# Gate projection of a float32 decoder trunk by one level of Strassen, gate and up with x loaded and weights streamed, their product transposed for down

## The chip, the cores and the metric

One core of one Trainium2 chip runs the whole program. The metric is device time in microseconds (us) from launch to end. TensorE is called PE, VectorE DVE, ScalarE ACT, and SyncE, which issues the loads, SP.

## The reference

Two layers of a decoder trunk on 256 positions, all in float32: four attention groups merged by one output projection, then a dense SwiGLU FFN with hidden width 5632. What matters here is the FFN:

```python
h = rms_norm(x, ffn_norm)                       # x: 256 x 2048
x = x + (silu(h @ w_gate) * (h @ w_up)) @ w_down    # 2048 -> 5632 -> 2048
```

## The kernel before

x lies transposed in SBUF, features on the partitions: X0 to X7 hold two feature tiles of 128 each, by 256 positions, and XS0 to XS7 hold the same, times the norm's gain, split into a high and a low part. Every float32 product is made of three products of such parts in PE's fp32r mode: high weight by high x, high weight by low x, low weight by high x.

The weights come from HBM in the order of use as tiles `raw` of 128x2048 (1 MB; L208 issues the load, three buffers). Each is split in two halves of 1024 columns: ACT rounds a half to `wh` (L216), DVE subtracts to get `wl` (L217). wh and wl have four buffers each.

In the FFN the weights are stationary. `proj_pair` makes two output tiles of 128 features by 256 positions: for each of the 16 feature tiles and each output tile it issues a matmul of 512 columns (wh on high and low x at once) and one of 256 (wl on high x), both from L233. They gather in a PSUM tile `acc` (two buffers); gate's and up's are put together by `pair` (L252 on ACT, L254 on DVE) and scaled by the norm's factor r_x; the silu and the product with up follow, and the result is split into the tiles h. `down` is the same `proj_pair` over 8 tiles h, whose two halves DVE adds to X (L258, L259). The hidden width is done in chunks of 8, 8, 8, 8, 8 and 4 times 128, each chunk's down after the next chunk's gate and up; the last 4 tiles and the output projection of attention's last group go through `last_out`, which uses the PSUM tiles `att` (four banks) and adds at L661.

A scheduler orders each engine's instructions from its own timeline when the program is built; on the chip every engine takes its list strictly in order.

Of the kernel before, what the change touches and what calls it, by code (L numbers as in the profile page):

```python
# [8 lines left out]
F32 = mybir.dt.float32  # L9
# [18 lines left out]
RAW_B, W_B, H_B, Q_B4, OG_B, T2, SG = 3, 4, 7, 4, 1, 3, 3  # L28
CH = [8, 8, 8, 8, 8, 4]
# [71 lines left out]

def pack_weights(w_in, w_uq, w_ukv, w_out, w_gate, w_up, w_down):
    us = []
    for l in range(DEPTH):
        m = w_in[l]
        us += quad_units(m, Q_LAT) + quad_units(m, KV_LAT)
        misc = np.zeros((D, 128), np.float32)
        misc[:, :64] = m[:, K_ROPE:K_ROPE + 64]
        misc[:, 64:68] = m[:, F_C:F_C + 4]
        us.append(unit(misc, 0, 16, 0, 128))  # L110

        def qkv(q0, k0, v0):
            r = []
            for c0 in (q0, q0 + 256, k0, k0 + 256):
# [19 lines left out]
        def gu(c):  # L134
            f0, r = 128 * sum(CH[:c]), []
            for f in range(f0, f0 + 128 * CH[c], 256):
                r += pair_units(w_gate[l], f) + pair_units(w_up[l], f)
            return r

        def dn(c):  # L140
            n = CH[c]
            cols = 2048 // n
            return [unit(w_down[l], sum(CH[:c]), n, c0, cols) for c0 in range(0, D, cols)]

        us += gu(0)
        for c in range(1, len(CH)):
            us += gu(c) + dn(c - 1)
        us += dn(len(CH) - 1)
    return np.concatenate([u.reshape(-1) for u in us])

# [16 lines left out]
def trunk(ctx: ExitStack, tc: tile.TileContext, x_d, w_d, sm_d, c_d, out_d):  # L167
# [4 lines left out]
    rawp = ctx.enter_context(tc.tile_pool(name="rawp", bufs=RAW_B))  # L172
    wp = ctx.enter_context(tc.tile_pool(name="wp", bufs=W_B))
    gp = ctx.enter_context(tc.tile_pool(name="gp", bufs=1))
    hp = ctx.enter_context(tc.tile_pool(name="hp", bufs=H_B))
    qp = ctx.enter_context(tc.tile_pool(name="qp", bufs=Q_B4))
# [6 lines left out]
    X = [cp.tile([128, 2, S], F32, name=f"X{i}") for i in range(8)]  # L183
    XS = [cp.tile([128, 2, 2, S], F32R, name=f"XS{i}") for i in range(8)]
    gp.tile([128, LINE], F32, name="gap")
# [14 lines left out]
    def load(n=2048, pieces=1, step=1024, before=None):  # L200
# [4 lines left out]
        for o in range(0, n, w):  # L205
            if before is not None:
                before(o // w)
            dma[0] = nc.sync.dma_start(raw[:, o:o + w], src[:, o:o + w])  # L208
        hs = []
# [75 lines left out]
    def proj_v(src, nk):  # L285
        acc = Acc()
        for k0 in range(0, nk, 4):
            blk = load()
            for kk in range(4):
                x = src(k0 + kk)  # L290
                wh, wl = blk(kk * 512, 512)
                last = k0 + kk == nk - 1
                for t in range(2):
                    o = acc.t[:, t].rearrange("p a b -> p (a b)")
                    ts = slice(t * 128, t * 128 + 128)
                    acc.mm(t, o, x[:, 0, ts], wh, False)
                    acc.mm(t, o, x[:, 0, ts], wl, False)
                    acc.mm(t, o, x[:, 1, ts], wh, last)
        return [acc.t[:, t].rearrange("p a b -> p (a b)") for t in range(2)]
# [13 lines left out]
    def rsq(tot, n, name, more=None):  # L313
        ps = attp.tile([128, 512], F32, name="att")
        if more is None:
            hl = tp.tile([128, 2, S], F32R, name="ss_hl", tag="hl", bufs=1)
# [10 lines left out]
        r0 = tp.tile([128, S], F32, name="rq_r", bufs=1)  # L327
# [40 lines left out]
    def softmax_heads(qk_mm, vt, scale, mask, o):  # L368
        st = []
        for h in range(4):  # L370
            s = tp.tile([128, 384], F32, name="sm_s", bufs=4)
# [19 lines left out]
        for s in st:  # L391
# [3 lines left out]
            p = tp.tile([128, 384], F32, name="sm_p", bufs=4)  # L395
# [35 lines left out]
    def stick_heads(qt, kt, vt, o):  # L431
        zs, es = [], []
        for h in range(4):
# [5 lines left out]
            z = tp.tile([128, 384], F32, name="sm_s", bufs=4)  # L439
# [3 lines left out]
        for z in zs:  # L443
            e = tp.tile([128, 384], F32, name="sm_p", bufs=4)
# [5 lines left out]
        for z, e in zip(zs, es):  # L450
            rc = attp.tile([128, 512], F32, name="att")
            hl = tp.tile([128, 2, 384], F32R, name="e_hl", bufs=1)
# [21 lines left out]
    for l in range(DEPTH):  # L474
# [53 lines left out]
        rope = {}  # L528
        for nm, c0, r in (("c", C_COS, rx), ("s", C_SIN, rx), ("pc", C_PCOS, rx), ("ps", C_PSIN, rx)):
            rope[nm] = tp.tile([128, S], F32, name="rope_" + nm, bufs=1)  # L530
            V.tensor_mul(rope[nm], cst[:, c0:c0 + S], r)
# [6 lines left out]
        kpe = []  # L538
        for j in range(2):
            t = tp.tile([128, S], F32, name=f"kpe{j}", bufs=1)  # L540
            V.memset(t, 0.0)
            kpe.append(t)
# [48 lines left out]
        og = qp.tile([128, 4, S], F32, name="og", bufs=OG_B)  # L591
# [3 lines left out]
        rope["qc"] = tp.tile([128, S], F32, name="rope_qc", tag="rope_pc", bufs=1)  # L595
        V.tensor_mul(rope["qc"], cst[:, C_PCOS:C_PCOS + S], rq)
        rope["qs"] = tp.tile([128, S], F32, name="rope_qs", tag="rope_ps", bufs=1)
        V.tensor_mul(rope["qs"], cst[:, C_PSIN:C_PSIN + S], rq)
        qpe = tp.tile([128, 2, S], F32, name="qpe", bufs=1)
# [9 lines left out]
        og = qp.tile([128, 4, S], F32, name="og", bufs=OG_B)  # L609
# [7 lines left out]
        cum_hl = tp.tile([128, 2, S], F32R, name="cum_hl", tag="hl", bufs=1)  # L617
# [8 lines left out]
        og = qp.tile([128, 4, S], F32, name="og", bufs=OG_B)  # L626
# [18 lines left out]
        og = qp.tile([128, 4, S], F32, name="og", bufs=OG_B)  # L645
# [21 lines left out]

        last_act = [None]

        def gate_up(n):  # L670
            hs = [hp.tile([128, 2, 2, S], F32R, name="h") for _ in range(n // 2)]
            for p in range(n // 2):
                pg = proj_pair(xk, KT, 8).pair()
                g = tp.tile([128, 2, S], F32, name="ff_g", tag="t2", bufs=T2)
                V.tensor_mul(g, pg, b2(rf))
                last_act[0] = A.activation(g, g, AF.Silu)
                pu = proj_pair(xk, KT, 8).pair()
                u = tp.tile([128, 2, S], F32, name="ff_u", tag="t2", bufs=T2)
                V.tensor_mul(u, pu, b2(rf))
                V.tensor_mul(u, u, g)  # L680
                split(hs[p], u)
            return lambda k: hs[k // 2][:, k % 2]

        srcs = [gate_up(CH[0])]
        for c in range(1, len(CH)):
            srcs.append(gate_up(CH[c]))
            if c + 1 == len(CH):
                with tc.issue_after(last_act[0].ins):
                    A.preload_act_table_set(LNEXP)
            for p in range(8):  # L690
                proj_pair(srcs[c - 1], 8, 8).add_to(X[p])
        nxt = (l + 1) * SM_L + SM_ATT if l + 1 < DEPTH else None
        last_out(srcs[-1], nxt)
# [15 lines left out]
def build(n_w):  # L709
    import concourse.bacc as _bacc  # L710
    nc = _bacc.Bacc("TRN2", target_bir_lowering=False, num_devices=1)
# [27 lines left out]
```

## Time and profile before

| | |
|---|---|
| median of 3 runs | 2278.14 us (2277.81 to 2279.25) |
| the profiled execution | 2278.91 us |
| its span, first to last instruction | 2277.0 us |
| PE busy | 2258.4 us |
| DVE busy | 1538.0 us |
| ACT busy | 1107.9 us |
| loads | 415.57 MB read, 183 GB/s over the span |

The span is what the trace covers; the profiled execution's own time is 1.9 us longer, and the median lies 0.8 us below it. An engine's busy time says how much of the span it worked, not whether anything waited for it.

### The profile page before, as it was taken

The numbers are of one execution on the slowest core, as the hardware profiler recorded it, in microseconds if no ns is written. First come the engines' busy times: TensorE is split into PE (matmuls) and PEld (weight loads), VectorE is DVE, ScalarE is ACT, GpSimd is POOL, SyncE is SP. The second block draws the span as 40 slices with busy tenths as digits, with TensorE's granted clock in tenths as the row PEclk, the third lists the DMA queues.
The fourth block names the chain that finished last, engine by engine and source line by source line (L and its number), as shares of the span: only waits on it lengthen the run. The fifth ranks groups of instructions, "written<-read, shape, count | busy, mean of one in ns | idle before, by whom it ended". The sixth has DMA issues, their size and how long they took to land.

```text
span 2277.0 us, 32935 instructions
## 1 busy us (share of the span) xinstructions
PE 2258.4 (99%) x13462; PEld 2009.6 (88%) x13462; DVE 1538.0 (68%) x1951; ACT 1107.9 (49%) x1425; POOL 0.2 (0%) x4
## 2 busy tenths in 40 slices
PE   8999999999999999999999999999999999999997
PEld 8888889888888888888998988898888888888887
DVE  7876767766656666666777866686666666665666
ACT  6455555544444444444554545565444444444344
POOL 0000000000000000000000000000000000000000
PEclk9999999999999999999999999999999999999999
DMA  7444445555555555555555454455555555555553
GB/s 283 176 167 167 164 142 199 199 186 191 193 189 185 193 196 185 186 191 196 184 184 186 143 177 163 153 198 196 187 194 193 185 186 196 192 185 188 196 189 111
DMA packets 61638, 419.79 MB, mean 184 GB/s; under 512 B 6832, under 2 KB 7088, under 8 KB 14768
## 3 DMA queue, kind: packets, MB, share of 16 engines
q1 hardware_dynamic: 61344, 417.63, 51.5%
q8 instruction: 106, 1.74, 0.3%
q14 instruction: 44, 0.36, 0.0%
q10 hardware_dynamic: 144, 0.07, 0.0%
HBM read 415.57 MB, written 2.10 MB: 183 GB/s over the span
## 4 chain that ended last, share of the span: by engine, by line
PE 99%; DVE 0%; DMA 0%; ACT 0%; DVEq 0%; issue 0%; SPq 0%; ACTq 0%
PE acc L233 92%; PE att L233 4%; PE att L404 1%; PE att L394 0%; PE att L405 0%; PE att L413 0%; PE att L323 0%; DMA X<-in_x_dram 0%; DVE X L704 0%; PE att L411 0%; PE att L425 0%; PE att L435 0%; PE att L427 0%; PE att L632 0%; PE att L423 0%; PE att L437 0%
## 5 line engine op out<-in xcount | busy, mean ns | idle before, releaser
L217 DVE TENSOR_TENSOR wl<-raw,wh 128x1024 fp32r<-128x1024 f32 (+1 forms) x810 | 963.6, 1192 | 650.8 <-ACT wh L216 649.5
L216 ACT ACTIVATE wh<-raw 128x1024 fp32r<-128x1024 f32 (+1 forms) x810 | 838.4, 1036 | 1072.5 <-PE acc L233 943.0
L233 PE MATMUL acc<-XS,wh 128*128 128x512 f32 (+1 forms) x4160 | 1352.8, 377 | 6.4 <-ACT XS L347 6.4
L233 PE MATMUL acc<-XS,wl 128*128 128x256 f32 x3872 | 1085.9, 281 | 0.0
L233 PEld LDWEIGHTS acc<-XS,wh 128*128 128x128 f32 x4160 | 763.3, 188 | 153.1 <-ACT XS L347 6.4
L233 PEld LDWEIGHTS acc<-XS,wl 128*128 128x128 f32 x3872 | 728.7, 188 | 1.0
L233 PE MATMUL acc<-h,wh 128*128 128x512 f32 (+1 forms) x1824 | 608.1, 381 | 0.0
L233 PE MATMUL acc<-h,wl 128*128 128x256 f32 x1744 | 492.2, 282 | 0.0
L233 PEld LDWEIGHTS acc<-h,wh 128*128 128x128 f32 x1824 | 337.1, 188 | 65.0
L233 PEld LDWEIGHTS acc<-h,wl 128*128 128x128 f32 x1744 | 329.5, 189 | 0.3
L233 PE MATMUL acc<-wh,XS 128*128 128x512 f32 x384 | 122.0, 396 | 0.0
L258 DVE TENSOR_TENSOR X<-X,acc 128x512 f32<-128x512 f32 x96 | 65.9, 687 | 40.1 <-PE acc L233 40.1
L233 PE MATMUL att<-h,wh 128*128 128x256 f32 x512 | 89.8, 279 | 0.0
L233 PEld LDWEIGHTS acc<-wh,XS 128*128 128x128 f32 x384 | 72.1, 188 | 17.6
L233 PEld LDWEIGHTS att<-h,wh 128*128 128x128 f32 x512 | 78.0, 188 | 0.2
L254 DVE TENSOR_TENSOR hilo<-acc,lo 128x512 f32<-128x512 f32 x112 | 76.6, 684 | 0.2
L233 PE MATMUL acc<-wl,XS 128*128 128x512 f32 x192 | 75.3, 392 | 0.0
L233 PE MATMUL att<-h,wl 128*128 128x256 f32 x256 | 71.4, 279 | 0.0
L259 DVE TENSOR_TENSOR X<-X,acc 128x512 f32<-128x512 f32 x96 | 65.9, 686 | 2.7
L252 ACT ACTIVATE lo<-acc 128x512 f32<-128x512 f32 x112 | 64.8, 578 | 0.0
L233 PEld LDWEIGHTS att<-h,wl 128*128 128x128 f32 x256 | 48.1, 188 | 0.0
L233 PEld LDWEIGHTS acc<-wl,XS 128*128 128x128 f32 x192 | 36.1, 188 | 8.4
(147 smaller groups left out, 895.8 us busy)
## 6 DMA issues: line engine op xcount, KB each, us to landing
raw<-in_w_dram SPq DMA_DIRECT2D x364, 1024.0 KB, 4.8
raw<-in_w_dram SPq DMA_DIRECT2D x32, 768.0 KB, 4.3
raw<-in_w_dram SPq DMA_DIRECT2D x8, 512.0 KB, 7.0
X<-in_x_dram SPq DMA_DIRECT2D x8, 256.0 KB, 6.3
out_dram<-X SPq DMA_DIRECT2D x8, 256.0 KB, 2.4
cst<-in_const_dram SPq DMA_DIRECT2D x1, 1216.0 KB, 9.3
raw<-in_w_dram SPq DMA_DIRECT2D x4, 256.0 KB, 5.4
cst<-in_const_dram SPq DMA_DIRECT2D x1, 67.0 KB, 7.4
```

What stands on the lines that cost most here:

```text
L216: A.activation(wh[:, i:e], raw[:, o + i:o + e], AF.Copy)
L217: V.tensor_sub(wl[:, i:e], raw[:, o + i:o + e], wh[:, i:e].bitcast(F32))
L233: P.matmul(out, lhsT, rhs, start=bank not in self.started, stop=stop, skip_group_check=True)
L252: A.activation(tmp, self.t[:, :, 1, :], AF.Copy)
L254: V.tensor_add(out, self.t[:, :, 0, :], tmp)
L258: V.tensor_add(x, x, self.t[:, :, 0, :])
L259: V.tensor_add(x, x, self.t[:, :, 1, :])
L404: P.matmul(po[:, :S], vt[0][:, hs], p[:, :S], start=True, stop=False, skip_group_check=True)
```

## The change

The FFN's hidden width goes in 11 groups of 512 columns (NG) a layer. In gate and up, x is now the stationary operand and the weights stream, so that their results have positions on the partitions.

- **gate** (`ProjSW`): x and the weight tile are cut in two in both directions, and seven products with 256 streamed columns take the place of eight. For each of the 8 pairs of feature tiles PE issues 21 matmuls of 256 columns (seven products, three parts each). Their seven sums fill all four `att` banks. DVE first makes four sums of weight quarters a pair (L348, L351, L353) and splits them as well as the weights (L354, L356; ACT at L352, L355); so each pair has two tiles of 1024 to split where there was one. The sums of x that four of the seven need are made once a layer (L767 to L776, in tiles xs_sum). `out` puts the seven together (L377 to L384).
- **up** (`ProjV`): the weight tile streams in matmuls of 512 columns, three for each of 16 feature tiles and 2 blocks of positions.
- The silu takes the norm's factor as its scale (L796), and L798 multiplies it with up, straight from PSUM.
- **turn**: 8 PE transposes of 128x128 in float32 a group (L807) into an `acc` buffer, which are then split into h (L439 on ACT, L440 on DVE).
- **down** is as before (its adds are now L283 and L284), but spread by `down_after`: 4 of a chunk's 8 after each group from the third on, and 8 after the last. After an even group (numbered from 0) its `turn` follows the first down; an odd group's comes within the next gate. In group 0 up precedes gate; in the others their steps alternate.
- wh and wl have six buffers instead of four, and several small tiles share buffers.

```diff
-RAW_B, W_B, H_B, Q_B4, OG_B, T2, SG = 3, 4, 7, 4, 1, 3, 3
-CH = [8, 8, 8, 8, 8, 4]
+RAW_B, W_B, H_B, Q_B4, T2, SG = 3, 6, 7, 8, 3, 3
+NG = HID // 512
+def down_after(g):
+    if g < 2:
+        return []
+    if g == NG - 1:
+        return [(g // 2 - 1, range(8))]
+    return [(g // 2 - 1, range(4) if g % 2 == 0 else range(4, 8))]
+    class ProjSW:
+        def __init__(self, sums):
+            self.sums = sums
+            ps = [attp.tile([128, 2, S], F32, name="att") for _ in range(4)]
...
+        def step(self, k0):
+            raw = fetch()
+            for j in range(2):
...
+                V.tensor_add(t[:, :512].rearrange("p (a b) -> p a b", a=2),
+                             q[:, :512].rearrange("p (a b) -> p a b", a=2),
+                             q[:, 768:][:, None, :].to_broadcast([128, 2, 256]))
+                V.tensor_add(t[:, 512:768], t[:, :256], q[:, 256:512])
+                A.activation(hs[:, :768], q[:, :768], AF.Copy)
+                V.tensor_add(t[:, 768:], t[:, 512:768], q[:, 512:768])
+                V.tensor_sub(ls[:, :768], q[:, :768], hs[:, :768].bitcast(F32))
+                A.activation(ht, t, AF.Copy)
+                V.tensor_sub(lt, t, ht.bitcast(F32))
...
+                    P.matmul(p, xh, wh[:, c], start=first, stop=False, skip_group_check=True)
+                    P.matmul(p, xl, wh[:, c], start=False, stop=False, skip_group_check=True)
+                    P.matmul(p, xh, wl[:, c], start=False, stop=i == 7, skip_group_check=True)
+        def out(self):
...
+            A.activation(c11, p[1], AF.Copy)
+            V.tensor_add(c12, c11, p[6])
+            V.tensor_add(c11, c11, p[2])
...
+            V.tensor_add(c12, c12, p[3])
+            y = tp.tile([128, 4, 128], F32, name="x_sum", tag="sg", bufs=SG)
+            V.tensor_sub(y[:, 0], a21, a22)
+            V.tensor_sub(y[:, 1], y[:, 0], a11)
+            V.tensor_sub(y[:, 2], a11, a21)
+            V.scalar_tensor_tensor(y[:, 3], a12, -1.0, y[:, 1], op0=OP.mult, op1=OP.subtract)
+            yt = qp.tile([128, 4, 2, 128], F32R, name="xs_sum", tag="q4")
+            A.activation(yt[:, :, 0, :], y, AF.Copy)
+            V.tensor_sub(yt[:, :, 1, :], y, yt[:, :, 0, :].bitcast(F32))
-        def gate_up(n):
+        def gate_up(g, turn_last):
+            up = ProjV(xk, KT)
+            if g == 0:
+                for i in range(4):
+                    up.step(4 * i)
+            gate = ProjSW(sums)
+            for i in range(4):
+                gate.step(4 * i)
+                if g > 0:
+                    up.step(4 * i)
+                if i == 0 and turn_last is not None:
+                    turn_last()
+            hid = gate.out()
...
+        def turn(hid):
+            pt = accp.tile([128, 2, 2, S], F32, name="acc")
...
+            for n, (c, p) in enumerate((c, p) for c, ps in down_after(g) for p in ps):
+                down(c, p)
+                if n == 0 and g % 2 == 0:
+                    turn(hid)
+                    held = None
```

The first place where the order of instructions is shown is the step from up to down. On DVE of before, this is the first layer's step from the second chunk's last up to the first chunk's downs (acc_5405 is that up, hilo and ff_u its results, acc_5499 the first down):

```order
L254 TENSOR_TENSOR hilo_5492<-acc_5405,lo_5490 128x512
L679 TENSOR_TENSOR ff_u_5494<-hilo_5492,r_x_4001 128x512
L217 TENSOR_TENSOR wl_5593<-raw_5590,wh_5592 128x1024
L680 TENSOR_TENSOR ff_u_5494<-ff_u_5494,ff_g_5402 128x512
L258 TENSOR_TENSOR X0_83<-X0_83,acc_5499 128x512
L259 TENSOR_TENSOR X0_83<-X0_83,acc_5499 128x512
L217 TENSOR_TENSOR wl_5597<-raw_5590,wh_5596 128x1024
L217 TENSOR_TENSOR wl_5638<-raw_5635,wh_5637 128x1024
L258 TENSOR_TENSOR X1_84<-X1_84,acc_5544 128x512
L259 TENSOR_TENSOR X1_84<-X1_84,acc_5544 128x512
L217 TENSOR_TENSOR wl_5642<-raw_5635,wh_5641 128x1024
L217 TENSOR_TENSOR wl_5683<-raw_5680,wh_5682 128x1024
```

On DVE of the changed kernel the same place after group 4 (acc_6197 is its up, raw_6841 the next group's first gate weights, acc_6686 its turn, acc_6641 and acc_6701 the first two downs):

```order
L798 SCALAR_TENSOR_TENSOR ff_g_6626<-acc_6197,rxc_3984,ff_g_6626 128x512
L348 TENSOR_TENSOR w_sum_6843<-raw_6841 128x512
L348 TENSOR_TENSOR w_sum_6876<-raw_6841 128x512
L242 TENSOR_TENSOR wl_6795<-raw_6792,wh_6794 128x1024
L351 TENSOR_TENSOR w_sum_6843<-w_sum_6843,raw_6841 128x256
L351 TENSOR_TENSOR w_sum_6876<-w_sum_6876,raw_6841 128x256
L283 TENSOR_TENSOR X0_89<-X0_89,acc_6641 128x512
L242 TENSOR_TENSOR wl_6799<-raw_6792,wh_6798 128x1024
L353 TENSOR_TENSOR w_sum_6843<-w_sum_6843,raw_6841 128x256
L440 TENSOR_TENSOR h_6687<-acc_6686,h_6687 128x2x256
L353 TENSOR_TENSOR w_sum_6876<-w_sum_6876,raw_6841 128x256
L284 TENSOR_TENSOR X0_89<-X0_89,acc_6641 128x512
```

Behind the last products with up now stand four sums for the next gate and two splits of weights ahead of the first add to X0, and the second add stands behind two more sums, a split and half of the turn.

On PE of before, the end of that first down and the beginning of the second, with what a row waits for:

```order
L233 MATMUL acc_5499<-h_4006,wl_5507 128x256
L233 MATMUL acc_5499<-h_4006,wh_5506 128x512
L233 MATMUL acc_5499<-h_4006,wl_5507 128x256
L233 MATMUL acc_5544<-h_4003,wh_5547 128x512 [waits DVE_49]
L233 MATMUL acc_5544<-h_4003,wl_5548 128x256
L233 MATMUL acc_5544<-h_4003,wh_5547 128x512
L233 MATMUL acc_5544<-h_4003,wl_5548 128x256
```

And of the changed kernel, the end of the first down, the turn and the beginning of the second down:

```order
L258 MATMUL acc_6641<-h_6306,wl_6649 128x256
L807 MATMUL acc_6686<-cst_110,ff_g_6625 128x128 [waits DVE_49]
L807 MATMUL acc_6686<-cst_110,ff_g_6626 128x128 [waits Activation_49]
L807 MATMUL acc_6686<-cst_110,ff_g_6625 128x128
L807 MATMUL acc_6686<-cst_110,ff_g_6626 128x128
L807 MATMUL acc_6686<-cst_110,ff_g_6625 128x128
L807 MATMUL acc_6686<-cst_110,ff_g_6626 128x128
L807 MATMUL acc_6686<-cst_110,ff_g_6625 128x128
L807 MATMUL acc_6686<-cst_110,ff_g_6626 128x128
L258 MATMUL acc_6701<-h_5439,wh_6704 128x512 [waits DVE_49,PE_49]
L258 MATMUL acc_6701<-h_5439,wl_6705 128x256
```

The turn takes the other one of the two acc buffers, so that the second down's first matmul waits for a DVE row; that row is the second add to X0 (L284) above.

The second place is the start of the first FFN. On DVE of before, behind the adds of the output projection (L661) come the splits of x (L348), the squares' sums (L309) and the weights' splits (L217):

```order
L348 SCALAR_TENSOR_TENSOR XS4_95<-X4_87,sm_100,XS4_95 128x256 x2
L309 TENSOR_TENSOR sq_3965<-sq_3965,sq_3976 128x512
L661 TENSOR_TENSOR X6_89<-X6_89,att_3905 128x512
L348 SCALAR_TENSOR_TENSOR XS5_96<-X5_88,sm_100,XS5_96 128x256 x2
L661 TENSOR_TENSOR X7_90<-X7_90,att_3935 128x512
L217 TENSOR_TENSOR wl_4053<-raw_4050,wh_4052 128x1024
L309 TENSOR_TENSOR sq_3965<-sq_3965,sq_3979 128x512
L217 TENSOR_TENSOR wl_4057<-raw_4050,wh_4056 128x1024
L348 SCALAR_TENSOR_TENSOR XS6_97<-X6_89,sm_100,XS6_97 128x256 x2
L348 SCALAR_TENSOR_TENSOR XS7_98<-X7_90,sm_100,XS7_98 128x256 x2
```

On DVE of the changed kernel, from the first sums of x to the norm's last row; wl_4291 is split from the sums for the gate's third pair:

```order
L770 TENSOR_TENSOR x_sum_3991<-xg_3988 128x128
L772 TENSOR_TENSOR x_sum_3991<-xg_3988 128x128
L353 TENSOR_TENSOR w_sum_4320<-w_sum_4320,raw_4285 128x256
L771 TENSOR_TENSOR x_sum_3991<-x_sum_3991,xg_3988 128x128
L356 TENSOR_TENSOR wl_4291<-w_sum_4287,wh_4290 128x1024
L773 SCALAR_TENSOR_TENSOR x_sum_3991<-xg_3988,x_sum_3991 128x128
L415 TENSOR_TENSOR sq_3943<-rq_r_3975 128x256
L348 TENSOR_TENSOR w_sum_4355<-raw_4353 128x512
L416 SCALAR_TENSOR_TENSOR sq_3943<-sq_3943 128x256
L776 TENSOR_TENSOR xs_sum_3996<-x_sum_3991,xs_sum_3996 128x4x128
L351 TENSOR_TENSOR w_sum_4355<-w_sum_4355,raw_4353 128x256
L418 SCALAR_TENSOR_TENSOR r_x_3979<-sq_3943,rq_r_3975 128x256
```

The sums of x and those of the weights stand mixed in one list, and up to the last of the eight xs_sum rows 68 rows follow from wl_4291 on: 6 of 1024 elements a partition, 6 of 768, 13 of 512, 12 of 256, 29 of 128 and 2 small ones.

The third place is the end of ACT's list, the last norm; before:

```order
L701 ACTIVATE X6_89<-X6_89,sm_100 128x256 x2
L697 ACTIVATE sq_20215<-X7_90 128x512
L701 ACTIVATE X7_90<-X7_90,sm_100 128x256 x2
L326 ACTIVATE sq_20194<-sq_20194 128x256
L328 ACTIVATE rq_r_20239<-sq_20194 128x256
```

And in the changed kernel:

```order
L839 ACTIVATE X6_95<-X6_95,sm_109 128x256 x2
L835 ACTIVATE sq_21892<-X7_96 128x512
L839 ACTIVATE X7_96<-X7_96,sm_109 128x256 x2
L412 ACT_TABLE_LOAD
L412 ACTIVATE sq_21871<-sq_21871 128x256
L414 ACT_TABLE_LOAD
L414 ACTIVATE rq_r_21916<-sq_21871 128x256
```

Each of its last two functions, the logarithm and the exponential, now has a table load ahead of it. ACT's list holds 31 table loads, where it held 5; apart from these two, the added ones stand between the first layer's last silus and the second layer's first.

## Rows read from the trace of the kernel before

**Rows 1.** The page: busy time by engine, then shares of the chain that ended last.

```profile
PE 2258.4 (99%) x13462; PEld 2009.6 (88%) x13462; DVE 1538.0 (68%) x1951; ACT 1107.9 (49%) x1425; POOL 0.2 (0%) x4
...
PE 99%; DVE 0%; DMA 0%; ACT 0%; DVEq 0%; issue 0%; SPq 0%; ACTq 0%
```

**Rows 2.** Busy time by stretch: the two FFNs without their last parts.

```profile
core 0: us, PE busy (x) PEld busy (x) DVE busy (x) ACT busy (x) POOL busy (x), PEclk, DMA share, GB/s
...
421.70:1113.70 692.00, 692.00 (x3995) 610.58 (x3994) 440.17 (x463) 312.33 (x341) 0.00 (x0) 1.00 0.54 190
1548.60:2240.60 692.00, 692.00 (x3995) 610.58 (x3994) 440.21 (x463) 312.31 (x341) 0.00 (x0) 1.00 0.53 190
```

**Rows 3.** Chain of waits, in order of time: start, us, what.

```profile
381.00 22.40 PE att L233 x192
...
421.71 692.01 PE acc L233 x3992
...
1548.64 692.01 PE acc L233 x3992
```

**Rows 4.** Timeline of PE: values projection, x stationary, weights streamed (start, us, what).

```profile
146.41 0.63 PE L233 MATMUL acc<-wh,h 128*128 128x512 f32 x2
146.88 0.39 PE L233 MATMUL acc<-wl,h 128*128 128x512 f32 x1
```

**Rows 5.** Timeline of PE: transposes in the attention between 256-column matmuls.

```profile
141.30 0.49 PE L394 MATMUL att<-cst,sm_s 128*128 128x128 f32 x3
141.54 0.37 PE L233 MATMUL acc<-h,wh 128*128 128x256 f32 x1
141.75 0.38 PE L394 MATMUL att<-cst,sm_s 128*128 128x128 f32 x2
```

**Rows 6.** Timeline of DVE, when it is full.

```profile
398.13 1.22 DVE L217 TENSOR_TENSOR wl<-raw,wh 128x1024 fp32r<-128x1024 f32 x1
399.26 0.68 DVE L661 TENSOR_TENSOR X<-X,att 128x512 f32<-128x512 f32 x1
399.86 1.22 DVE L217 TENSOR_TENSOR wl<-raw,wh 128x1024 fp32r<-128x1024 f32 x1
401.00 0.87 DVE L348 SCALAR_TENSOR_TENSOR XS<-X,sm,XS 128x256 fp32r<-128x256 f32 x2
```

**Rows 7.** Groups by shape: busy us, mean ns, idle before.

```profile
L310 DVE TENSOR_TENSOR sq<-sq 128x256 f32<-128x256 f32 x17 | 7.2, 422 | 0.3
L389 DVE TENSOR_SCALAR sm_s<-sm_s,sm_ri 128x128 f32<-128x128 f32 x24 | 6.7, 280 | 0.1
```

**Rows 8.** Timeline of ACT: the first silu, idle time in brackets.

```profile
428.56 1.06 ACT L216 ACTIVATE wh<-raw 128x1024 fp32r<-128x1024 f32 x1 [1.23 <-PE acc L233]
429.64 1.28 ACT L676 ACT_TABLE_LOAD   x1
430.94 0.63 ACT L676 ACTIVATE ff_g<-ff_g 128x512 f32<-128x512 f32 x1
```

**Rows 9.** Timeline of ACT: the last norm.

```profile
2266.11 0.42 ACT L326 ACTIVATE sq<-sq 128x256 f32<-128x256 f32 x1 [0.74 <-DVE sq L325]
2266.56 0.42 ACT L328 ACTIVATE rq_r<-sq 128x256 f32<-128x256 f32 x1
```

**Rows 10.** Waits: engine, line, releaser; us in total, times, longest.

```profile
ACT wh L216 <- PE acc L233: 943.0, 632, 2.3
DVE wl L217 <- ACT wh L216: 649.5, 567, 4.0
```

**Rows 11.** Busy time by stretch: the start, and after the last matmul (columns as above).

```profile
6.30:12.40 6.10, 6.03 (x27) 5.79 (x28) 5.54 (x13) 6.10 (x15) 0.00 (x0) 1.00 1.04 399
12.40:18.50 6.10, 6.10 (x53) 6.10 (x53) 6.10 (x13) 6.10 (x15) 0.00 (x0) 1.00 1.04 401
...
2268.70:2277.00 8.30, 0.00 (x0) 0.00 (x0) 4.59 (x8) 0.00 (x0) 0.00 (x0) 0.50 0.68 253
```

**Rows 12.** The tile raw: from a load's issue to its landing.

```profile
DMA to landing us min/median/max: 3.6/4.8/8.0
```

More of the change, by code (lines that the diff above doesn't have):

```diff
@@ L183, in trunk @@
     X = [cp.tile([128, 2, S], F32, name=f"X{i}") for i in range(8)]
+    for p in (cp, gp0, gp, gp1):
+        p.tile([128, LINE], F32, name="gap")
     XS = [cp.tile([128, 2, 2, S], F32R, name=f"XS{i}") for i in range(8)]
-    gp.tile([128, LINE], F32, name="gap")
     sm = cp.tile([128, SM_N], F32, name="sm")
@@ L198, in trunk, with fetch @@
     dma = [None]
-    def load(n=2048, pieces=1, step=1024, before=None):
+    def fetch(n=2048, pieces=1, before=None):
         raw = rawp.tile([128, 2048], F32, name="raw")
@@ L208, in load @@
             dma[0] = nc.sync.dma_start(raw[:, o:o + w], src[:, o:o + w])
+        return raw
+    def load(n=2048, pieces=1, step=1024, before=None):
+        raw = fetch(n, pieces, before)
         hs = []
@@ L283, in proj_quad, with __init__ @@
         return acc.t
-    def proj_v(src, nk):
-        acc = Acc()
-        for k0 in range(0, nk, 4):
+    class ProjV:
+        def __init__(self, src, nk):
+            self.acc, self.src, self.nk = Acc(), src, nk
+            self.out = [self.acc.t[:, t].rearrange("p a b -> p (a b)") for t in range(2)]
+        def step(self, k0):
             blk = load()
             for kk in range(4):
-                x = src(k0 + kk)
+                x = self.src(k0 + kk)
                 wh, wl = blk(kk * 512, 512)
-                last = k0 + kk == nk - 1
+                last = k0 + kk == self.nk - 1
@@ L293, in proj_v @@
                 for t in range(2):
-                    o = acc.t[:, t].rearrange("p a b -> p (a b)")
                     ts = slice(t * 128, t * 128 + 128)
[L296 to L299, printed above, removed]
+                    self.acc.mm(t, self.out[t], x[:, 0, ts], wh, False)
+                    self.acc.mm(t, self.out[t], x[:, 0, ts], wl, False)
@@ L390, in softmax_heads @@
         pst = []
-        for s in st:
+        sp = tp.tile([128, 4, 384], F32, name="sm_p", tag="big", bufs=2)
+        for h, s in enumerate(st):
             pt = attp.tile([128, 512], F32, name="att")
@@ L666, in trunk @@
         rf = rsq(sumsq(X), D, "r_x")
-        last_act = [None]
-        def gate_up(n):
[L671 to L682, printed above, removed]
@@ new lines, in turn @@
+        def turn(hid):
+            pt = accp.tile([128, 2, 2, S], F32, name="acc")
+            hs = [hp.tile([128, 2, 2, S], F32R, name="h") for _ in range(2)]
+            for f in range(4):
+                for t in range(2):
+                    P.transpose(pt[:, f // 2, f % 2, t * 128:t * 128 + 128],
+                                hid[t][:, f * 128:f * 128 + 128], ident)
+            for p in range(2):
+                split(hs[p], pt[:, p])
+            hts.extend(hs)
+        hts = []
@@ L688, in trunk, with down @@
+        def down(c, p):
+            proj_pair(lambda k: hts[4 * c + k // 2][:, k % 2], 8, 8).add_to(X[p])
+        held = None
+        for g in range(NG):
+            hid = gate_up(g, None if held is None else (lambda v=held: turn(v)))
+            held = hid
+            if g == NG - 1:
                 with tc.issue_after(last_act[0].ins):
                     A.preload_act_table_set(LNEXP)
-            for p in range(8):
-                proj_pair(srcs[c - 1], 8, 8).add_to(X[p])
+            for n, (c, p) in enumerate((c, p) for c, ps in down_after(g) for p in ps):
+                down(c, p)
+                if n == 0 and g % 2 == 0:
+                    turn(hid)
+                    held = None
```

139 lines of the change are left out of this document (100 added, 39 removed).

## The prediction, made before the changed kernel ran

> **What bounds the kernel now.** The page first: PE is busy in 2258.4 of 2277.0 us, DVE in 68% and ACT in 49% of the span, and the chain that ended last is PE for 99% [rows 1]. The busy time by stretch then says where this holds: in both FFN stretches PE works 692.00 of 692.00 us, DVE 440 and ACT 312 [rows 2]. The chain of waits shows each stretch as one piece of PE without a break [rows 3], and the waits are the other way round: ACT stands 943.0 us for PE and DVE 649.5 us for ACT, both because buffers come free at PE's pace [rows 10]. So PE time saved is worth its full length, as long as DVE and ACT deliver in time; and DVE has 250 us to spare in such a stretch, on the average. The question for each part is therefore PE time first, and then the places where DVE is late.
>
> **Gate on PE.** In the FFN piece 3992 matmuls, half of 512 columns and half of 256, take 692.01 us, .3467 us for a pair; 192 of 256 columns take 22.40, .1167 each [rows 3]. Gate had 11 x 64 = 704 pairs a layer, 244.1 us. It gets 11 x 8 x 21 = 1848 matmuls of 256 columns, 215.6 us. For two layers: **-57.0**. This is sure to a microsecond if the short ones run here as they do there.
>
> **Up on PE.** The same 244.1 us a layer become 11 x 96 = 1056 matmuls of 512 columns. The values projection has this form: two start .47 us ahead of the third [rows 4], .235 each. Two parts of a pair would be .2311 (.3467 x 2/3), and I take .233: 246.0 us, **+4** for two layers; bounds -0.2 and +8.
>
> **Turns on PE.** 176 transposes. Among 256-column matmuls, three transposes and one such matmul take .45 us from start to start [rows 5]: (.45 - .117)/3 = .111 each, **+19.5**, .89 a turn. Bounds 17 and 21 by the reading of the starts.
>
> PE alone is thus 33.5 us shorter. The rest is waiting.
>
> **DVE's prices.** When it is full, a row of 1024 elements takes 1.13 us to the next one's start and one of 512 .60 [rows 6], that is .08 less than its duration. Rows of 256 and 128 last .42 and .28 [rows 7], so .34 and .20; scalar-tensor rows of 256 .39 [rows 6]; one of 768 I put between 512 and 1024, .87.
>
> **Steady steps.** A gate step and an up step give PE 42 x .1167 + 24 x .233 = 10.5 us. DVE has 2 x (.60 + .34 + .34 + .87 + 1.13) + 2 x 1.13 = 8.8 us, 9.9 by full durations: PE stays the bound there. The tile that both halves of a gate step are read from is held longer: a landing of 4.8 us [rows 12] and about 5 us of DVE make 10 for three buffers, which suffices. I price the steady part at 0.
>
> **First gate of a layer.** Here DVE has the sums of x on top of those of the weights, in one list. wl_4291 needs wh_4290, whose buffer is that of the last half tile of up: it comes free when PE ends up, 96 x .233 = 22.3 us after its start. ACT's 1.06 [rows 8] and .2 of signals make 23.7. From there the 68 rows to the last sum of x are 6 x 1.13 + 6 x .87 + 13 x .60 + 12 x .36 + 29 x .21 + .2 = 30.5 us with the prices above, and some 2 us for rows that wait for ACT in between: 56. PE then still has 15 matmuls, 1.75, so gate ends at 58; PE's own work would end at 22.3 + 19.7 = 42. That is 16 a layer, **+32**; bounds 12 (every row finds its operands) and 18 each.
>
> **Into the second group.** The next gate needs the four att banks, which `out` reads; the last of those reads stands in DVE's list some 7.2 us behind gate's end, and PE has 2.2 us of other work ahead. +5; once more about +1 into the third group, where DVE has caught up: two layers **+12**, bounds 4 and 14.
>
> **Even groups.** PE's second down waits for L284, which frees the acc buffer (the turn has the other). Count from PE's end of up. ACT can split the third down's second half only when up frees its buffer: 1.26. Then DVE's list runs: that wl, 2.45; two L798, 3.75; two sums of 512, 4.95; a wl, 6.1; two of 256, 6.8; L283, 7.5; a wl, 8.6; .34, half a turn .64, .34, and L284 ends at 10.7. PE is there after the first down's 16 pairs, 5.55, and the turn, .88: 6.4. A stall of 4.3 us after groups 4, 6 and 8; after group 2, where less is mixed in, 3.5, and after 10, without a next gate, .8: 17.2 a layer, **+34**; bounds 15 (half of the sums done earlier) and 45. What is queued behind that matmul is all of PE's work. After odd groups the second down waits for L798 at 3.75, before 5.55, and the third for L284 at 9.95, before 11.1: nothing.
>
> **The last norm.** Ahead of the last output ACT runs logarithm and exponential back to back [rows 9]; now each has a table load before it, of 1.28 us [rows 8], and PE has nothing left to cover it. With .4 for the small products that turn the norm's factor into a column, **+3**; bounds 1.6 (one load runs while ACT waits for DVE anyway) and 4. The other 24 loads lie where ACT works half its time; 0, at most 6. The Trainium skill (ScalarE: Activation LUTs, What ACT_TABLE_LOAD costs) puts a load with its drain at about 2.7 us, by which this term would be 5.7. The row shows 1.28 and the next function .02 us behind it, so the sum goes by the row.
>
> **The sum.** -57 + 4 + 19.5 + 32 + 12 + 34 + 3 = +47.5: a span of 2324.5. The profiled execution lies 1.9 above its span, and the median .8 below that execution: **2326 us**. With each term at its ends, 2284 and 2361; they won't all lie at one end, so I give this case 2300 to 2350 and a chance of .70.
>
> **The rivals.**
> - *The stalls are hidden.* If DVE runs further ahead than I count, only PE's work and the tail are left: 2277 - 33.5 + 3, so 2247 us, faster by 1.4%. For it: DVE has 36% of the FFN free [rows 2]. Against it: both engines wait for buffers that PE frees [rows 10], so they cannot run ahead past six halves, and the sums of x have no earlier place. It turns into a gain as soon as all stalls are below 31 us. Chance .06. Half of my stalls gives 2290, slower by 0.5%; another .06.
> - *The clock falls with each stall.* In the first 6.1 us of work PE does 27 matmuls, in the next 53, all of one kind and fed alike [rows 11]: it begins at half the rate, 1.2 of 2.4 GHz if that is the clock, and 3 us are lost. The granted clock is again .50 after the last matmul [rows 11]. Some 15 stalls of over 3 us would cost up to 3 us each once more: 2371. Against it: the FFN of before is one piece without such a gap [rows 3], so nothing shows one to bring the clock down. Chance .10. The Trainium skill (TensorE: Matmul & The Clock Gate, HAM oscillation — how this bites in real kernels) says that a kernel which waits a few us in every step begins every step cold; no row here shows it inside the kernel.
> - *The loads or DVE become the bound in every step.* Steps have 10.5 us for about 10. If a landing takes 6.5 us (the longest took 8.0 [rows 12]), each of 80 steps loses .9: 2398. For it: a gate tile is read by eight DVE rows and two of ACT. Chance .08.
>
> **Chances and range.** Likeliest .70, clock .10, bound in every step .08, hidden .06, half .06. The range must leave out the two outer cases: 2288 to 2372. Within 0.2%, 4.6 us, is about what a measurement of this kernel can't tell from no change; only a time between "hidden" and "half" falls there. Of the .12 that these two hold I put .07 below it, .03 within and .02 above; everything else is slower. Faster .07, same .03, slower .90.
>
> **What the trace would show.** 256-column matmuls at .117 and 512 at .233 in the FFN; transposes at .11; PE standing for DVE rows of sums for 16 us in each first gate; one gap of 4 us ahead of the second down after groups 4, 6 and 8, released by L284; and two loads in the last norm. I am wrong if the gaps ahead of the second down are missing, if the first gate ends about 42 us after up's start, or if a granted clock of .50 stands inside the FFN.

## The result: 2368.57 us, slower by 4.0%

The median of four runs is 2368.57 us (2366.64 to 2369.71) against 2278.2 before, ratio 1.0395 (95% interval 1.0377 to 1.0413). The profiled execution has a span of 2367.2 us, 90.2 more than before. It lies in the range of 2288 to 2372, near its upper end; the forecast was half the size, and the likeliest case, 2300 to 2350, was missed.

The page, busy time and the shares of the chain that ended last, as in [rows 1]:

```profile
PE 2268.4 (96%) x13822; PEld 2028.1 (86%) x13822; DVE 1872.5 (79%) x2717; ACT 1271.2 (54%) x1653; POOL 0.2 (0%) x4
...
PE 90%; DVE 6%; ACT 2%; issue 1%; DMA 0%; DVEq 0%; ACTq 0%; SPq 0%
```

PE is no longer the whole chain: DVE and ACT hold 8% of it. Where the time lies is read from the four blocks of 192 matmuls that end each half layer; their starts in the chain of waits (start, us, what), of the kernel before and then of the changed one:

```profile
381.00 22.40 PE att L233 x192
...
1113.71 22.40 PE att L233 x192
...
1507.93 22.40 PE att L233 x192
...
2240.64 22.41 PE att L233 x192
```

```profile
390.29 22.40 PE att L258 x192
...
1154.76 22.40 PE att L258 x192
...
1566.28 22.40 PE att L258 x192
...
2328.91 22.41 PE att L258 x192
```

Before, the first block began at 381.00, and each FFN took 732.7 us up to the next. Now attention of the first layer takes 9.3 us more, the first FFN 31.8, attention of the second layer 17.3, the second FFN 29.9, and the end 1.9. So 61.7 us lie in the FFN, where 44.5 were forecast, and **26.6 in attention, where nothing was**.

The starts of PE's matmuls divide this further: a start-to-start time over .117 us (256 columns) or .231 (512) by more than .35 is counted as a wait, by .06 to .35 as a slow matmul. In the FFNs that gives 67.9 us of waits and 28.4 of slow matmuls, where before had none of either. Of the waits 36.0 belong to the even groups, ahead of the turn and of the second down, 31.9 to the first gates. Stretches of the changed kernel (columns as in [rows 2]): the first gate, a steady step, the wait after group 6, and the time just after it.

```profile
434.90:469.50 34.60, 24.25 (x174) 22.57 (x173) 33.48 (x77) 22.46 (x38) 0.00 (x0) 0.90 0.26 92
743.97:754.44 10.47, 10.47 (x67) 9.41 (x67) 9.19 (x13) 5.85 (x7) 0.00 (x0) 1.00 0.57 200
841.40:845.90 4.50, 0.53 (x5) 0.29 (x3) 4.50 (x10) 1.78 (x3) 0.00 (x0) 0.81 0.35 89
845.90:849.00 3.10, 3.02 (x9) 2.66 (x10) 0.54 (x1) 0.00 (x0) 0.00 (x0) 0.50 0.69 291
```

The steady step is as forecast: 10.47 us, PE busy throughout, DVE 9.19. In the wait DVE works all of 4.50 us. After it PE is busy again, but with a granted clock of .50, 1.2 of 2.4 GHz, and 9 matmuls in 3.1 us: the price of such a wait is more than its length. The timeline of PE around such a wait (start, us, what, idle before in brackets), after group 4:

```profile
704.79 0.28 PE L258 MATMUL acc<-h,wl 128*128 128x256 f32 x1
704.91 1.04 PE L807 MATMUL acc<-cst,ff_g 128*128 128x128 f32 x8
710.18 0.47 PE L258 MATMUL acc<-h,wh 128*128 128x512 f32 x1 [4.23 <-DVE X L284]
...
711.29 0.42 PE L258 MATMUL acc<-h,wl 128*128 128x256 f32 x1
711.50 0.63 PE L258 MATMUL acc<-h,wh 128*128 128x512 f32 x1
```

And DVE in the same stretch:

```profile
701.84 1.40 DVE L798 SCALAR_TENSOR_TENSOR ff_g<-acc,rxc,ff_g 128x512 f32<-128x512 f32 x2
703.33 1.29 DVE L348 TENSOR_TENSOR w_sum<-raw 128x512 f32<-128x512 f32 x2
704.54 1.22 DVE L242 TENSOR_TENSOR wl<-raw,wh 128x1024 fp32r<-128x1024 f32 x1
...
706.35 0.68 DVE L283 TENSOR_TENSOR X<-X,acc 128x512 f32<-128x512 f32 x1
706.95 1.22 DVE L242 TENSOR_TENSOR wl<-raw,wh 128x1024 fp32r<-128x1024 f32 x1
...
708.42 0.68 DVE L440 TENSOR_TENSOR h<-acc,h 128x512 fp32r<-128x512 f32 x1
...
709.35 0.68 DVE L284 TENSOR_TENSOR X<-X,acc 128x512 f32<-128x512 f32 x1
```

DVE has no pause here. PE's last turn matmul starts at about 705.7, the second add ends at 710.0, and PE goes on at 710.18.

Attention's longest new gap in the first layer (timeline of all engines, some rows). A projection's last matmul starts at 251.11; the next projection, 64 matmuls from 251.23 on, ends at about 266; a third is to begin:

```profile
251.11 0.28 PE L258 MATMUL acc<-XS,wl 128*128 128x256 f32 x1
251.23 0.39 PE L258 MATMUL acc<-XS,wh 128*128 128x512 f32 x1
...
265.85 0.28 PE L409 MATMUL att<-ss_hl,exact 128*128 128x256 f32 x1
...
266.96 0.40 ACT L412 ACTIVATE sq<-sq 128x256 f32<-128x256 f32 x1
...
267.39 0.42 ACT L414 ACTIVATE rq_r<-sq 128x256 f32<-128x256 f32 x1
267.71 0.58 ACT L277 ACTIVATE lo<-acc 128x512 f32<-128x512 f32 x1
...
268.56 0.68 DVE L279 TENSOR_TENSOR hilo<-acc,lo 128x512 f32<-128x512 f32 x1
...
269.30 0.50 PE L258 MATMUL acc<-XS,wh 128*128 128x512 f32 x1 [3.17 <-DVE hilo L279]
```

PE's third projection needs the acc buffer of the first, which lo and hilo empty. That one was complete at 251.4, but in ACT's list its lo stands behind a norm's logarithm and exponential, which need PE's L409 of 265.85: it is read 16 us later, at 267.71. In the second layer the same gap has two table loads in it and is 5.64 us long:

```profile
1439.55 1.28 ACT L412 ACT_TABLE_LOAD   x1
...
1441.28 1.28 ACT L414 ACT_TABLE_LOAD   x1
...
1444.26 0.80 PE L258 MATMUL acc<-XS,wh 128*128 128x512 f32 x1 [5.64 <-DVE hilo L279]
```

### The profile page after: what moved, and what is told of

Read it like the earlier page. It is cut to its first block, busy times and chain, and to the rows that moved or that the text cites. A ratio compares the mean times of both kernels' runs of the same rounds, so it can differ in the third digit from the quotient of the medians.

```text
span 2367.2 us, 34828 instructions
## 1 busy us (share of the span) xinstructions
PE 2268.4 (96%) x13822; PEld 2028.1 (86%) x13822; DVE 1872.5 (79%) x2717; ACT 1271.2 (54%) x1653; POOL 0.2 (0%) x4
## 4 chain that ended last, share of the span: by engine, by line
PE 90%; DVE 6%; ACT 2%; issue 1%; DMA 0%; DVEq 0%; ACTq 0%; SPq 0%
PE acc L258 67%; PE att L369 6%; PE att L370 6%; PE att L371 5%; PE att L258 4%; DVE wl L242 1%; DVE w_sum L348 1%; ACT wh L241 1%; PE acc L807 0%; PE att L492 0%; DVE w_sum L351 0%; DVE ff_g L798 0%; DVE w_sum L353 0%; PE att L501 0%; DVE wl L356 0%
## 5 line engine op out<-in xcount | busy, mean ns | idle before, releaser
L242 DVE TENSOR_TENSOR wl<-raw,wh 128x1024 fp32r<-128x1024 f32 (+1 forms) x634 | 744.5, 1181 | 284.2 <-ACT wh L241 282.3
L258 PE MATMUL acc<-h,wh 128*128 128x512 f32 (+1 forms) x1824 | 626.7, 389 | 32.5 <-DVE X L284 31.7
L258 PE MATMUL acc<-wh,XS 128*128 128x512 f32 x1792 | 576.4, 395 | 0.5 <-ACT wh L241 0.5
L258 PE MATMUL acc<-h,wl 128*128 128x256 f32 x1744 | 499.0, 286 | 0.0
L258 PEld LDWEIGHTS acc<-h,wh 128*128 128x128 f32 x1824 | 345.3, 192 | 103.0 <-issue 31.9
L258 PE MATMUL acc<-XS,wh 128*128 128x512 f32 (+1 forms) x1344 | 385.2, 352 | 19.6 <-DVE hilo L279 11.3
L258 PEld LDWEIGHTS acc<-wh,XS 128*128 128x128 f32 x1792 | 337.4, 188 | 75.1 <-ACT wh L241 0.7
L258 PE MATMUL acc<-wl,XS 128*128 128x512 f32 x896 | 353.6, 395 | 0.0
L258 PEld LDWEIGHTS acc<-h,wl 128*128 128x128 f32 x1744 | 337.4, 193 | 1.0
L258 PE MATMUL acc<-XS,wl 128*128 128x256 f32 x1056 | 303.0, 287 | 0.0
L258 PEld LDWEIGHTS acc<-XS,wh 128*128 128x128 f32 x1344 | 237.4, 192 | 53.2 <-DVE hilo L279 11.9
L355 ACT ACTIVATE wh<-w_sum 128x1024 fp32r<-128x1024 f32 x176 | 186.5, 1060 | 175.2 <-PE acc L258 72.3
L356 DVE TENSOR_TENSOR wl<-w_sum,wh 128x1024 fp32r<-128x1024 f32 x176 | 215.1, 1222 | 25.6 <-ACT wh L355 19.1
L354 DVE TENSOR_TENSOR wl<-raw,wh 128x768 fp32r<-128x768 f32 x176 | 167.6, 952 | 47.4 <-ACT wh L352 47.3
L258 PEld LDWEIGHTS acc<-XS,wl 128*128 128x128 f32 x1056 | 202.2, 192 | 0.8
L352 ACT ACTIVATE wh<-raw 128x768 fp32r<-128x768 f32 x176 | 148.5, 843 | 97.9 <-PE acc L258 94.8
L370 PE MATMUL att<-wh,xs_sum 128*128 128x256 f32 x704 | 197.1, 283 | 3.0 <-DVE xs_sum L776 3.0
L258 PEld LDWEIGHTS acc<-wl,XS 128*128 128x128 f32 x896 | 168.9, 188 | 35.5
L369 PE MATMUL att<-wh,xs_sum 128*128 128x256 f32 x704 | 194.6, 282 | 2.2 <-ACT xs_sum L775 1.6
```

The source lines that it names most:

```text
L242: V.tensor_sub(wl[:, i:e], raw[:, o + i:o + e], wh[:, i:e].bitcast(F32))
L258: P.matmul(out, lhsT, rhs, start=bank not in self.started, stop=stop, skip_group_check=True)
L352: A.activation(hs[:, :768], q[:, :768], AF.Copy)
L354: V.tensor_sub(ls[:, :768], q[:, :768], hs[:, :768].bitcast(F32))
L355: A.activation(ht, t, AF.Copy)
L356: V.tensor_sub(lt, t, ht.bitcast(F32))
```

## The experiments

The theory after the result: (a) the even groups' waits come from the turn's taking the second acc buffer, and each brings the clock down; (b) the first gate is bound by DVE; (c) attention is longer because rq_r, the norm's tile, shares the ring of lo and hilo, and because of the table loads. The main rival: DVE is late as a whole, and a wait that is taken away comes back at the next row.

**The turn held.** Diff:

```diff
-                if n == 0 and g % 2 == 0:
+                if n == 0 and g == NG - 1:
```

> The turn of every group but the last is held until the next group's gate, as that of odd groups already is; nothing else changes. If the second down waits for the acc buffer because the turn has taken the other one, all gaps of 4 us ahead of the second down go (36 us over both layers), and with them the matmuls at half rate behind them (17 us): about 2315 us. If DVE is simply late there, whoever holds the buffer, the gaps move to the next row that needs DVE and the time stays above 2350. If the half rate behind a gap is not caused by the gap, 36 us go and 17 stay: 2332.

Measured: 2320.98 us, ratio to before 1.0186 (1.0171 to 1.0201). The span is 2315.7, 51.5 less (47.6 by the medians: this kernel's four runs lie 6.3 us apart, and the profiled one is the fastest). The FFNs' waits fall by 36.5 us, 32 of them at the even groups and the rest at the first gates, and their slow matmuls by 13.9; in the list of waits, PE's for the second add (31.7 us in 10 waits, "PE acc L258 <- DVE X L284") is down to 1.5 us in two. DVE's work is the same (1870.6 us busy, for 1872.5), so it was the buffer, not DVE's load.

**The gap filled.** Diff, behind the even groups' turn:

```diff
+                    if 0 < g < NG - 1:
+                        fill = attp.tile([128, 2, S], F32, name="att")
+                        v = hts[4 * c][:, 0].rearrange("p a b -> p (a b)")
+                        hold[0] = tr
+                        for i in range(15):
+                            with tc.issue_after(hold[0].ins):
+                                hold[0] = P.matmul(fill.rearrange("p a b -> p (a b)"), v[:, :128],
+                                                   v, start=i == 0, stop=i == 14,
+                                                   skip_group_check=True)
```

(tr is the turn's last transpose, and the next down's first matmul is issued after the last of the fifteen.)

> The changed kernel with 15 needless matmuls of 512 columns (3.5 us) put on PE between the turn and the second down after groups 2, 4, 6 and 8; their result is not used, and everything else, the wait for the second add to X0 included, stays. If the gap of 4 us is what brings the clock down, the slow matmuls behind these eight gaps (16 us) go although nothing is done earlier: about 2353 us, in spite of the added work. If the slow matmuls have another cause, or the needless ones delay the wait's end, 2367 or more.

Measured: 2355.15 us, 1.0337 (1.0320 to 1.0355), 13.4 less than the changed kernel with 28 us of needless work in it. PE in that run, after group 6, and the stretch that follows:

```profile
835.13 3.71 PE L841 MATMUL att<-h 128*128 128x512 f32 x15
839.42 0.47 PE L261 MATMUL acc<-h,wh 128*128 128x512 f32 x1 [0.59 <-DVE X L288]
839.73 0.28 PE L261 MATMUL acc<-h,wl 128*128 128x256 f32 x1
839.84 0.40 PE L261 MATMUL acc<-h,wh 128*128 128x512 f32 x1
```

```profile
839.40:846.00 6.60, 6.58 (x38) 5.84 (x39) 2.15 (x4) 1.66 (x2) 0.00 (x0) 1.00 0.32 133
```

The second down still waits for the second add, but runs at full rate: the granted clock is 1.00, and 38 matmuls fit in 6.6 us, .35 us a pair. The slow matmuls are gone behind seven of the eight gaps and stay, 1.65 us, where PE waited 2.26 us ahead of the turn itself, which the filling doesn't cover. DVE's rows stand in the same order through the whole first layer, where the FFN is 10.6 us shorter (in the second, where the list came out differently at the first gate, 2.9); so it is PE's idle time that brings the clock down, not anything on DVE.

**The norm's column late.** Diff:

```diff
-        rfc = rcol(rf, "rxc")
-        rfn = tp.tile([128, 2], F32, name="rfn", bufs=1)
-        V.tensor_scalar(rfn, rfc, -1.0, None, op0=OP.mult)
...
+            if g == 0:
+                rfc = rcol(rf, "rxc", accp.tile([128, 2, 2, S], F32, name="acc"))
+                rfn = tp.tile([128, 2], F32, name="rfn", bufs=1)
+                V.tensor_scalar(rfn, rfc, -1.0, None, op0=OP.mult)
+                cols.extend((rfc, rfn))
+            rfc, rfn = cols
             hid = gate.out()
```

> The small products that turn the FFN norm's factor into a column are made after the first gate, in an acc buffer, so that PE need not wait for the factor before that gate. If DVE is the bound through the whole first gate, as the prediction had it, the waits of 5.6 and 7.5 us come back later in the same gate and its end hardly moves: 2362 to 2368. If the wait for the factor adds to the rest, it goes with the slow matmuls behind it, 17 us: 2351.

Measured: 2370.74 us, 1.0401 (1.0386 to 1.0417): nothing gained, as in the expectation's first case, and 3 us above its bounds. The changed kernel's PE waited 12.7 us in all for that factor (L418); in this run such a wait is absent, and these are there instead (waits: engine, line, releaser; us, times, longest), with DVE's busy time from up's end to the first gate's last matmul (columns as above):

```profile
PE att L370 <- DVE xs_sum L775: 11.0, 11, 2.1
PE att L369 <- ACT xs_sum L774: 8.8, 6, 2.9
```

```profile
434.60:473.00 38.40, 28.15 (x172) 25.29 (x171) 38.14 (x84) 25.89 (x41) 0.00 (x0) 0.83 0.30 99
```

DVE works 38.14 of 38.40 us. The wait moved down DVE's list, as a bound on DVE has it: here the rival holds. It is a balance, though: the first FFN is 4.3 us shorter and the second 6.7 longer, since waits in the FFNs fall by 6 us in all while slow matmuls grow by 9.

**The late table load.** Diff:

```diff
-            if g == NG - 1:
-                with tc.issue_after(last_act[0].ins):
-                    A.preload_act_table_set(LNEXP)
...
                     turn(hid)
                     held = None
+                    if g == NG - 1:
+                        with tc.issue_after(last_act[0].ins):
+                            A.preload_act_table_set(LNEXP)
```

(last_act is now the split of the turn. In the changed kernel the load for both functions stands between two silus, whose own table is then loaded once more; on ACT:)

```profile
1107.31 1.28 ACT L824 ACT_TABLE_LOAD   x1
...
1109.71 1.28 ACT L796 ACT_TABLE_LOAD   x1
1111.01 0.51 ACT L796 ACTIVATE ff_g<-ff_g,rfn 128x256 f32<-128x256 f32 x1
```

(The second layer has the same at 2283.86: besides the last norm's two, this added load too stands outside the stretch between the two layers' silus.)

> The load of the table for logarithm and exponential is put behind the split of the last turn, so that it can no longer stand between two silus; 5 table loads are left of 31. If loads cost time wherever a norm's chain is waited for, the longer gaps of the second layer (7.5 against 5.6, 5.8 against 3.3, 2.6 against none) and 2.6 us of the last norm go, some 10 to 12 us with the slow matmuls behind them: 2357. If they are hidden except in the last norm, as the prediction had it: 2366.

Measured: 2358.69 us, 1.0353 (1.0337 to 1.0368); the span is 11.3 less, 7.5 of it in the second layer's attention and about 2 at the end. In the second layer the gaps of 2.6 and 5.8 us become none and 3.3, those of the first; 5 of the 31 loads are left.

**The norm's own buffer.** Diff:

```diff
-        r0 = tp.tile([128, S], F32, name="rq_r", tag="t2", bufs=T2)
+        r0 = tp.tile([128, S], F32, name="rq_r", bufs=1)
```

> The norm's tile rq_r has a buffer of its own again and does not share the ring of the tiles lo, hilo and ff_g; nothing else changes. If attention is longer because lo's buffer, and with it its place in ACT's list, stands behind a norm's logarithm and exponential, the gaps of 3.3 us in the first layer and 5.8 in the second go with the slow matmuls behind them: some 12 us, 2356. If it is the table loads or the other shared buffers that make attention longer, less than 4 us go: 2365 or more.

Measured: 2344.91 us, 1.0293 (1.0276 to 1.0310); the span is 25.4 less, twice what was expected. The first layer's attention is as long as before the change (the first block starts at 381.16), the second's within 2.1 us. ACT around the same norm (timeline):

```profile
248.18 0.58 ACT L277 ACTIVATE lo<-acc 128x512 f32<-128x512 f32 x1
...
262.79 0.58 ACT L277 ACTIVATE lo<-acc 128x512 f32<-128x512 f32 x1
263.26 0.41 ACT L412 ACTIVATE sq<-sq 128x256 f32<-128x256 f32 x1
263.70 0.42 ACT L414 ACTIVATE rq_r<-sq 128x256 f32<-128x256 f32 x1
```

Both lo stand ahead of the logarithm and the exponential again, .6 us behind the ends of their projections. The shorter gaps of attention (1.4 us and less in the first layer, 2.6 and less in the second) are all but gone too, where the expectation counted only the longest; which row stood behind which at each of them is not shown. With lo ahead, even the table loads of the second layer, still in this kernel, cost little.

**Three repairs together** (turn, table load, buffer; the diffs above).

> Turn held, late table load and the norm's own buffer together. If the three causes are separate, their gains add, less the share that table loads had in the second layer's longest attention gap: 2367 - 50 - 25 - 7 of span, about 2285 us. If they hide one another, that is if DVE is late anyway, 2300 or more.

Measured: 2297.31 us, 1.0083 (1.0068 to 1.0098); the span is 2295.8, 10.8 more than the 2285 expected. Alone, the three take 51.5, 11.3 and 25.4 us off the span, 88.2 in sum, and together 71.4. The table loads' gain in attention lies in the gaps that the buffer closes anyway: the second layer's attention is 395.6 us with both and 396.3 with the buffer alone. Another 5 us lie in the FFNs, which gain 45 us here and 50 with the turn alone. The list is made anew with every edit, and PE now waits 4.2 us for L799 (the products with up) and 6.1 for L379; but 5 us is also less than the runs of the held turn differ by, so no cause is shown for it.

**The first gate without Strassen**, on top of the three. Diff:

```diff
         def gate(g, i):
+            if g == 0:
+                return unit(w_gate[l], 4 * i, 4, 512 * g, 512)
             return quarters(w_gate[l], 4 * i, 512 * g)
...
-            gate = ProjSW(sums)
+            gate = ProjSW(sums) if g > 0 else ProjV(xk, KT, True)
```

(ProjV's True puts its sums into two att banks; silu and product with up then read them, without `out`.)

> The three repairs, and in each layer's first group gate is done without Strassen (24 matmuls of 512 columns a weight tile, two att banks), so that no weight sums stand beside the sums of x; the sums of x are still made. PE's own work grows by 2.8 us a layer. If the first gate's waits (20 us a layer with the step into the second group and the slow matmuls) come from DVE having both kinds of sums at once, 2 x 17 us go: 2251. If the sums of x alone keep DVE behind, the waits move to the second group: 2280 or more.

Measured: 2265.21 us, 0.9942 (0.9927 to 0.9957). The waits in each FFN fall from 18.7 and 17.9 us to 4.1, of which 3.2 are now for the norm's factor. The time is 14 above the 2251 expected, because the three repairs themselves came out higher: against them it is 32.1 less, for 34. So it was both kinds of sums at once; the sums of x alone are hidden.

**That, and the norm's column late.**

> As the run with the first gate unsplit, and the norm's column is made behind that gate. DVE is no longer the bound there, so that the wait for the norm's factor should now add: if so, some 5 us a layer less than that run, about 2243; if the factor is in time there anyway, the same as that run.

Measured: **2257.78 us, 0.9909 (0.9894 to 0.9923)**, .9% below the kernel before. What gained nothing while DVE was the bound now gains 7.4 us, where 10 were expected. Its first FFN without the block before it, 698.60 us with PE busy in 696.99 (before, 732.7 - 22.4 = 710.3):

```profile
403.50:1102.10 698.60, 696.99 (x4209) 619.86 (x4208) 601.26 (x827) 381.33 (x446) 0.00 (x0) 1.00 0.54 193
```

**No Strassen at all**, with the three repairs. Diff:

```diff
-            return quarters(w_gate[l], 4 * i, 512 * g)
+            return unit(w_gate[l], 4 * i, 4, 512 * g, 512)
...
-        for i in range(8):
+        for i in range(0):
             xg = tp.tile([128, 2, S], F32, name="xg", tag="sg", bufs=SG)
...
-            gate = ProjSW(sums)
+            gate = ProjV(xk, KT, True)
```

> The three repairs, and no Strassen at all: gate like up, x loaded and weights streamed, in every group, with two att banks for it and two for the turn; no sums of x or of weights. PE gets 57 us of work back against the run with the three repairs, and loses that run's waits of 20 us a layer at the first gate: 2285 + 57 - 40, about 2302. If those waits have another source than the sums, 2340. If the sums also cost PE time in the steady steps, less than 2295.

(The turn goes into the two other att banks.) Measured: 2309.33 us, 1.0135 (1.0118 to 1.0152). The expectation was made from 2285 for the three repairs; against their span as measured, 2295.8, it is 11.8 more. At .232 a matmul, gate as up costs 1056 x .232 - 215.6 = 29.4 us a layer more, 58.8; waits and slow matmuls in the FFNs fall by 46.9; that leaves 11.9. So the waits came from the sums, and the steady steps lose nothing to them. (The turn's banks changed too; but the unsplit first gate, which left them alone, took 28.4 of the 36.6 us of waits.) Against the best version it is 51.6 us slower, and 10/11 of 58.8 is 53: Strassen is worth nearly its full PE time once DVE is in time.

## Why the prediction was right in sign and short in size

- **PE's own work** was forecast at -33.5 us. A steady step takes 10.47 us, so that a 512-column matmul takes (10.47 - 42 x .1167)/24 = .232: up costs 1.8 us where 4 were forecast. A turn takes .79 us from its first start to the next matmul's where nothing waits, forecast .89: 17.4 us for 19.5. With gate's -57.0 and .8 for the small products of the norm's column that is about -37.
- **The first gate.** It was to end 58 us after up's start. In the first layer up starts at 412.5 and the gate's last matmul at 469.4: 57; in the second it is 60. The row wl_4291, forecast 23.7 us after up's start, came after 24.0 (436.56). DVE was busy in 33.48 of the 34.60 us from up's end, and with the late column in 38.14 of 38.40, with a gate that ended 61 and 65 us after up's start. First gate and step into the second group were forecast at 32 + 12; measured are 31.9 of waits and 11.6 of slow matmuls, 43.5. The sum agrees, but its parts were others. Slow matmuls, some of them hidden by DVE, stand in for a wait that was put too high; and some 13 us of the waits lie ahead of the gate, for the norm's factor, whose small products the prediction priced at .4 of PE's work and not as a row to wait for. That the terms agree so closely is in part luck.
- **The even groups.** Forecast 4.3 us after groups 4, 6 and 8, 3.5 after 2 and .8 after 10; measured 4.2 to 4.4, 5.0 and 3.8 (with a wait ahead of the turn), and .9: 36.0 us for 34. Holding the turn took 32 of these 36 us away.
- **The clock: a step that failed.** It stood among the rivals with a chance of .10 and not in the sum, since nothing showed a gap to bring it down. A granted clock of .50 inside the FFN was one of the prediction's own signs of being wrong, and it stands there (845.90:849.00). It was not a rival but came on top: 16.8 us behind the even groups' gaps, 1.6 to 2.5 each (12 to 16 slow matmuls), where the rival had put 3. The filled gap shows it by itself. (The 3 us were read from the first 6.1 us, for which [rows 11] shows a granted clock of 1.00; only the row after the last matmul shows .50.)
- **Attention: the other step that failed.** "The other 24 loads lie where ACT works half its time; 0, at most 6", and the buffers that attention's tiles now share were not priced at all. It cost 26.6 us. The buffer run shows that 24.3 of it go with one tile's place; the loads' share, 7.5 in the second layer's attention, shrinks to .7 where lo stands ahead of the norm. That ACT is idle on the average said nothing of a row that stands behind another in ACT's list.
- **The last norm.** +1.9 us for +3. The rows show the two loads at the 1.28 us of [rows 8] each, the function .01 behind; the first falls in the .74 us for which ACT stood for DVE before [rows 9]:

```profile
2353.66 1.28 ACT L412 ACT_TABLE_LOAD   x1
2354.95 0.42 ACT L412 ACTIVATE sq<-sq 128x256 f32<-128x256 f32 x1
2355.39 1.28 ACT L414 ACT_TABLE_LOAD   x1
2356.68 0.42 ACT L414 ACTIVATE rq_r<-sq 128x256 f32<-128x256 f32 x1
```

The Trainium skill (ScalarE: Activation LUTs, What ACT_TABLE_LOAD costs) has about 2.7 us for a load with its drain. No drain is seen here, and the term is nearer to the row's.

The Trainium skill (TensorE: Matmul & The Clock Gate, HAM oscillation — how this bites in real kernels) says that a kernel which waits a few us in every step begins every step cold. This trace agrees for the even groups: behind the waits of 3.8 to 5 us the matmuls are slow, here once in such a group and not in every step.

The sum of what was missed: 26.6 of attention and 16.8 of clock, 43.4, against a gap between forecast and span of 90.2 - 47.5 = 42.7. The other terms (-3.5 of PE's work, -.5, +2 and -1.1) come to -3.1, so that 2.4 us are in no term. That the loads or DVE bind in every step, the steady step excludes; that the stalls are hidden, the waits of 67.9 us.

That the range held the time is luck: it reached to 2372 and so took in the clock rival, with 45 us of slow matmuls on top of the forecast. The time came there by 16.8 us of them and by 26.6 us of attention, for which the sum had nothing. Two sums of the prediction don't come out of its terms, and nothing hangs on them: all terms at their ends give about 2282 and 2349 (2355 with the other loads), not 2284 and 2361, and half of the stalls about 2287, not 2290.

## What to carry to other kernels

Saving work on the engine that bounds a kernel pays only as far as its helpers' queues deliver at the few places where two kinds of extra work meet; count the rows of the helper's list at these places, since its average share says nothing. Price a wait of several us of the matmul engine as its length and a stretch at half rate behind it. When buffers are merged to make room, look at what each shared ring puts behind what on the in-order engines, also in stages that the change doesn't touch.

## What the runs showed of the hardware that had not been expected

A gap of about 4 us on PE is followed by 12 to 16 slow matmuls, with the granted clock down to .50, which cost 1.6 to 2.5 us; with 3.5 us of needless matmuls in the gap they are gone behind seven of eight such gaps, and the granted clock stays at 1.00. So idle PE time of a few us can be cheaper when it is filled with work that nobody needs: 13 us over eight gaps here.

The granted clock also fell behind shorter gaps. At the end of the first layer's first gate PE waits .9, .7, .4 and 2.2 us between 469.4 and 476.25; then:

```profile
475.50:482.30 6.80, 6.05 (x28) 6.05 (x29) 6.61 (x11) 2.31 (x5) 0.00 (x0) 0.50 0.73 270
```
